# Squares summed in pairs, another order of norm and values, solves of three heads at a time: one core, one decoder trunk

## The chip, the cores and the metric

The kernel runs on one core of one Trainium2 chip. A core has a matrix engine (PE; its weight loads are listed apart as PEld), a vector engine (DVE), a scalar engine (ACT), a general engine (POOL) and an engine that here only issues transfers (SP). The first four work on tiles in SBUF; PE writes its results to PSUM, from where DVE and ACT read them. The metric is the device time of one launch in microseconds; less is better.

## The reference

The program is a two-layer decoder trunk over 512 positions of 1024 values, batch 1, in float32. Cut to what is computed:

```
mem_n = rms_norm(mem, ln_mem)                       # 256 memory tokens
for layer in (0, 1):
    h = rms_norm(x, ln_mix[layer])
    mem_k, mem_v = split(mem_n @ w_mem_kv[layer])   # both layers read the same memory
    if layer == 0:  mix, mem_q = gated_deltanet(h)  # 6 heads, chunked WY form
    else:           mix, mem_q = window_attention(h @ w_q, shared_k, shared_v)
    x = x + concat(mix, memory_attention(mem_q, mem_k, mem_v)) @ w_out[layer]
    x = x + swiglu(rms_norm(x, ln_ffn[layer]))
    if layer == 0:  shared_k, shared_v = rope / split of rms_norm(x, ln_kv) @ w_kv
return rms_norm(x, ln_final)
```

Here `rms_norm(x, g) = x * rsqrt(mean(x^2) + eps) * g`. The gated-DeltaNet layer needs, for every head and chunk of positions, the solution of a unit lower triangular system: `(I + lower) sol = rhs`. The kernel inverts the triangular matrices in blocks.

## The kernel before

Activations lie transposed: tile k of x holds 128 of the 1024 channels on the partitions and the 512 positions along the row, eight tiles in all. A large product is done in float32 by parts: each operand is split into a rounded high part and the rest (`split`: the high part is a copy on ACT, the low part a subtraction on DVE), and `mm3` issues three matmuls, high by high, high by low, low by high. A 128x1024 weight comes by one transfer (`wraw`), is split into `whi` and `wlo`, and feeds 24 matmuls. Weights wait in two raw buffers and three split ones (`whi`, `wlo`). Nobody writes the order of the engines by hand: a scheduler sets it from the program's order, from a model of the costs and from the buffers that are free, and each engine then works through its queue in that order. PSUM has eight banks, shared out by tag: in the first layer three `pj` (projections), two `g` and three `sc`.

The stages that the change touches are these.

*Early stage* (`mem_and_norm`, L279 to L363). Memory and weights are loaded, memory is split with its gain, `keys(0)` projects the first layer's memory keys (two tiles, 48 matmuls of 256 columns), `memory_stats` gets the norm of memory, `values(0)` projects the values (48 matmuls), `rstd_of` gets the norm of x, `norm` scales the eight tiles of x on DVE and splits them into `h` and `l`, and `keys(1)`, `values(1)` do the second layer's projections, which are kept in DRAM. Then `gates` projects two small gates from `h` and `l` (16 matmuls with `wabs`), and the projections of the first layer with a causal convolution begin (`conv_tile`).

`rstd_of` (L210) takes the sum of squares over the 1024 channels: each tile is squared on ACT into one of four `sq` buffers, and a plain float32 matmul with a matrix of ones adds it up over partitions and tiles in one `g` bank; two ACT steps (logarithm, exponential) make the inverse root. It runs once over memory (256 columns) and once over x (512).

*Solves* (`solve`, L650). For one head it turns four chunks' inverses of 32x32 blocks into inverses of 64 and then 128: products into an `sc` bank, a copy `Y` out of it on DVE, products with it into the same bank, and scalings by -1 into `X` and `Tt` on DVE. It does the two pairs of 32-blocks after each other and then the pair of 64-blocks. `values(heads)` (L560) inside `gdn` calls it for each of three heads and then does the three heads' value projections; the order is values of heads 0 to 2, their scan over four chunks, values of heads 3 to 5, their scan.

*End* (`ffn`, L897 to L909, and `final`, L1038). The last output tile of the last layer is done in two halves of 256 positions. For each half, x is added, squared on ACT, added on DVE to the running sum of squares `acc`, summed by one matmul with ones, turned into `rstd` by two ACT steps, and then `final` multiplies the eight tiles with gain and `rstd`: six on DVE (`fin`, one instruction each), two (`k0 == 4`) with the gain on ACT and `rstd` on POOL. Four output transfers per half follow.

Of the kernel before, what the change touches and what calls it, by code (L numbers as in the profile page):

```python
# [9 lines left out]
F32 = mybir.dt.float32  # L10
# [13 lines left out]
NC = 4  # L24
# [61 lines left out]
class Builder:  # L86
# [123 lines left out]
    def rstd_of(self, tiles, pool, out, after=None):  # L210

        ps = self.bank("g")[:, :tiles[0].shape[1]]
        for k, x in enumerate(tiles):
            sq = self.t(pool, [P, x.shape[1]], F32, "sq", 4)
            ins = self.square(sq, x)
            if after is not None:
                self.nosync(ins, after)
            self.mm(ps, self.ones, sq, k == 0, k == KD - 1)
        self.rsqrt(out, ps, D)
# [59 lines left out]
    def mem_and_norm(self, ep):  # L279
# [9 lines left out]
        for k in range(0, KD, 2):  # L289
            nc.sync.dma_start(mem[:, k:k + 2, :], a["memT"][:, k:k + 2, :])  # L290
            if k < 4:
                s = slice(k // 2 * T, (k // 2 + 1) * T)
                nc.sync.dma_start(raw[0][:, s], a["wmk"][0, 0][:, s])
        raw += [early(s) for s in (a["wmk"][0, 1], a["wmv"][0, 0], a["wmv"][0, 1])]
        self.fetch_constants()
        for k in range(KD):
            self.split_gain(mem[:, k, :], self.gain(G_MEM, k), mh[:, k, :], ml[:, k, :])
        for k in range(0, KD, 2):
            nc.sync.dma_start(x[:, k:k + 2, :], a["xT"][:, k:k + 2, :])
        wab = self.t(ep, [P, KD, 12], F32, "wab")  # L300
        nc.sync.dma_start(wab, a["wab"])
# [7 lines left out]
        def keys(layer):  # L309
            ps, ks = [], []  # L310
            for m in range(2):
                w = self.weight(None, nc.vector, raw[4 * layer + m], 1 if m + layer else 2)
                ps.append(self.bank("pj")[:, :ML])
                for k in range(KD):
                    self.mm3(ps[m], w, k, (mh[:, k, :], ml[:, k, :]), k == 0, k == KD - 1)
# [10 lines left out]
        def values(layer):  # L326
            vs = []
            w = [self.weight(None, nc.vector, raw[4 * layer + 2 + j]) for j in range(2)]
            for j in range(2):
                ps = self.bank("pj")[:, :ML]  # L330
                s = slice(j * P, (j + 1) * P)
# [21 lines left out]
        self.memK = keys(0)  # L353
        self.memV = values(0)
        self.rstd_of([x[:, k, :] for k in range(KD)], ep, xr)
        norm()
        w = self.wab = self.t(ep, [P, KD, 64], F32R, "wabs")
        nc.gpsimd.memset(w.bitcast(F32), 0.0)
# [96 lines left out]
    def gdn(self, gp):  # L455
# [104 lines left out]
        def values(heads):  # L560
            for h in heads:
                self.solve(gp, h, N[h], X, Tt[h])
            for h in heads:
                v = self.conv_tile(2 * H + h, self.t(gp, [P, T], F32, "qv", 5))
# [35 lines left out]

        first, second = range(0, 3), range(3, H)
        values(first)
        scan(first)
# [45 lines left out]

    def solve(self, gp, h, N, X64, Tt):  # L650

        X = X64[:, h * NC:(h + 1) * NC, :]
        B = BASE
        part = lambda ps, a, w: ps[:, a * w * NC:(a + 1) * w * NC].rearrange("p (c m) -> p c m", c=NC)
        ps = self.bank("sc")
        yx, rx, rt = (part(ps, a, B) for a in range(3))
        y = self.t(gp, [P, NC, B], F32, "Y32", 2)
        for a, b in ((slice(0, B), slice(B, 2 * B)), (slice(2 * B, 3 * B), slice(3 * B, 4 * B))):
            first = a.start == 0
            for c in range(NC):  # L660
                self.mm(yx[b, c, :], N[a, c, b], X[a, c, 0:B])
            self.nc.vector.tensor_copy(y[b], yx[b])
            for c in range(NC):
                if first:
                    self.mm(rx[b, c, :], Tt[b, c, b], y[b, c, :])
                self.mm(rt[a, c, :], y[b, c, :], Tt[b, c, b])
            if first:
                self.ts(X[b, :, 0:B], rx[b], -1.0, ALU.mult)
            self.ts(Tt[a, :, b], rt[a], -1.0, ALU.mult)
        ps = self.bank("sc")  # L670
        B = 2 * BASE
        yx, rt = (part(ps, a, B) for a in range(2))
        y = self.t(gp, [P, NC, B], F32, "Y64", 2)
        a, b = slice(0, B), slice(B, 2 * B)
        for c in range(NC):
            self.mm(yx[b, c, :], N[a, c, b], X[a, c, :])
        self.nc.vector.tensor_copy(y[b], yx[b])
        for c in range(NC):
            self.mm(rt[a, c, :], y[b, c, :], Tt[b, c, b])
        self.ts(Tt[a, :, b], rt[a], -1.0, ALU.mult)  # L680

# [180 lines left out]
    def ffn(self, fp, xp, layer, h, apool, rope=False):  # L862
# [34 lines left out]
        if tail < KD:  # L897

            w = {m: [down(m, j, n, pool=fp if m == KD - 1 and tail < KD - 1 else None) for j, n in ((0, 6), (6, 5))] for m in range(tail, KD)}
            for t in (slice(0, T // 2), slice(T // 2, T)):  # L900
                acc = self.acc[:, t]
                for m in range(tail, KD):
# [4 lines left out]
                    self.tt(nc.vector, x, ps, x, ALU.add)  # L907
                    self.accumulate(xp, acc, x, m, acc)
                self.final(fp, acc, t)  # L909

# [126 lines left out]

    def final(self, fp, acc, t):  # L1038

        nc = self.nc  # L1040
        self.rstd_from(acc, t)
        r = self.rstd[:, t]
        rows = self.a["out"].rearrange("(k p) t -> p k t", p=P)
        for k0 in range(0, KD, 2):
            o = self.t(fp, [P, 2, T // 2], F32, f"fin{k0}", 2)
            for k in (k0, k0 + 1):
                x, y = self.x[k][:, t], o[:, k - k0, :]
                if k0 == 4:
                    self.copy(y, x, scale=self.gain(G_FIN, k))
                    self.tt(nc.gpsimd, y, y, r, ALU.mult)  # L1050
                else:
                    self.stt(y, x, self.gain(G_FIN, k), r, ALU.mult, ALU.mult)
            nc.sync.dma_start(rows[:, k0:k0 + 2, t], o)
# [59 lines left out]
```

## Time and profile before

| | us |
|---|---|
| median of 3 runs | 1239.17 |
| lowest, highest | 1237.04, 1240.69 |
| profiled execution, its time | 1240.29 |
| profiled execution, its span | 1238.5 |
| PE busy | 1202.3 (97%) |
| DVE busy | 651.6 (53%) |
| ACT busy | 523.4 (42%) |
| POOL busy | 92.9 (8%) |
| PE idle before the first matmul | 6.0 |

The profile shows one execution. Busy time counts an instruction from start to modelled end, so neighbours on PE overlap in it; the distance from one start to the next is what an instruction costs in a stream. The mean granted clock of PE over the execution is 0.992 of full speed: it is 1.00 for most of the time and 0.50 in a few stretches. A line in a row can be that of a helper (L143 is every matmul, L150 every two-operand product or sum on POOL and DVE, L131 and L137 the ACT functions and copies), so the tiles' names tell the stage. In the chain of waits each piece is followed back from the last instruction to what released it; a name after `<-` in brackets is what ended an engine's idle time.

### The profile page before, as it was taken

Reading aid. Unit: us, or ns where it says so; the run is one execution under the profiler, and the core shown is the slowest. Engines: PE = TensorE matmul, PEld = TensorE weight load, DVE = VectorE, ACT = ScalarE, POOL = GpSimd, SP = SyncE. Lnnn points to the kernel's source line nnn. Section 1 sums busy time; section 2 is a strip of 40 time slices with the busy share of each in tenths; the row PEclk is TensorE's granted clock in tenths of the full one; section 3 lists DMA queues with packets and bytes.
Section 4 is the critical chain, followed back from the end, with each engine's and each line's share of the span. In section 5 each row is a group of like instructions: output and inputs, shape, how many; then the busy total and the mean of one; then the engine's idle time right before and its main releaser. Section 6 shows DMA issues by size and latency. Waiting matters only on the chain.

```text
span 1238.5 us, 15507 instructions
## 1 busy us (share of the span) xinstructions
PE 1202.3 (97%) x5963; PEld 984.7 (80%) x5963; DVE 651.6 (53%) x1116; ACT 523.4 (42%) x972; POOL 92.9 (8%) x63
## 2 busy tenths in 40 slices
PE   7899999999999999999999999989999999999996
PEld 6677777877888888888888888878888888888885
DVE  4554686667954433334435789967344333344344
ACT  6468375337442322222333557774323222223332
POOL 0120000000011110011110000000111100111001
PEclk9899999999999999999999999999999999999998
DMA  7332643223432223333333553304333233333232
GB/s 273 118 119 55 199 123 95 86 85 109 139 102 92 96 77 96 117 102 94 94 83 94 152 152 82 86 18 122 100 95 93 78 98 115 102 97 91 83 94 79
DMA packets 56798, 129.48 MB, mean 105 GB/s; under 512 B 15452, under 2 KB 19188, under 8 KB 56724
## 3 DMA queue, kind: packets, MB, share of 16 engines
q1 hardware_dynamic: 56724, 128.49, 34.8%
q8 instruction: 47, 0.77, 0.3%
q14 instruction: 27, 0.22, 0.1%
HBM read 113.12 MB, written 6.96 MB: 97 GB/s over the span
## 4 chain that ended last, share of the span: by engine, by line
PE 83%; ACT 5%; DVE 4%; DMA 2%; issue 1%; SPq 0%; DVEq 0%; ACTq 0%
PE pj L143 51%; PE g L143 25%; PE sc L143 5%; ACT sm L131 1%; DVE wlo L150 1%; PE g L147 1%; PE pt L147 1%; ACT whi L137 1%; ACT DT L131 1%; ACT h L137 0%; DVE fin L153 0%; DVE kn L153 0%; DMA wraw<-in_wq 0%; DVE l L153 0%; DMA wraw<-in_wout 0%
## 5 line engine op out<-in xcount | busy, mean ns | idle before, releaser
L137 ACT ACTIVATE whi<-wraw 128x1024 fp32r<-128x1024 f32 (+2 forms) x213 | 207.3, 975 | 546.4 <-PE pj L143 332.0
L143 PE MATMUL pj<-h,whi 128*128 128x512 f32 (+1 forms) x960 | 377.0, 394 | 2.1 <-ACT h L137 2.0
L143 PE MATMUL pj<-h,wlo 128*128 128x512 f32 (+1 forms) x960 | 374.8, 391 | 1.9 <-DVE wlo L150 1.9
L143 PE MATMUL pj<-l,whi 128*128 128x512 f32 (+1 forms) x960 | 375.6, 391 | 0.0
L150 DVE TENSOR_TENSOR wlo<-wraw,whi 128x1024 fp32r<-128x1024 f32 (+2 forms) x213 | 238.9, 1123 | 144.5 <-ACT whi L137 144.1
L143 PEld LDWEIGHTS pj<-h,whi 128*128 128x128 f32 x960 | 180.3, 188 | 39.0 <-ACT h L137 3.1
L143 PEld LDWEIGHTS pj<-h,wlo 128*128 128x128 f32 x960 | 180.5, 188 | 38.3 <-DVE wlo L150 2.6
L143 PEld LDWEIGHTS pj<-l,whi 128*128 128x128 f32 x960 | 180.6, 188 | 36.5 <-issue 1.0
L143 PE MATMUL g<-h,wlo 128*128 128x512 f32 x408 | 159.3, 390 | 0.6 <-DVE wlo L150 0.6
L143 PE MATMUL g<-l,whi 128*128 128x512 f32 x408 | 159.4, 391 | 0.0
L143 PE MATMUL g<-h,whi 128*128 128x512 f32 x408 | 159.2, 390 | 0.0
L150 POOL TENSOR_TENSOR fg<-fg,rstd 128x512 f32<-128x512 f32 x44 | 75.5, 1717 | 1009.6 <-ACT fg L131 1009.6
L150 DVE TENSOR_TENSOR fu<-g,fg 128x512 f32<-128x512 f32 x44 | 30.4, 691 | 142.6 <-PE g L143 139.9
L143 PEld LDWEIGHTS g<-h,wlo 128*128 128x128 f32 x408 | 76.8, 188 | 16.8 <-DVE wlo L150 1.0
L143 PEld LDWEIGHTS g<-l,whi 128*128 128x128 f32 x408 | 76.9, 188 | 16.0
L143 PEld LDWEIGHTS g<-h,whi 128*128 128x128 f32 x408 | 76.7, 188 | 15.8
L150 DVE TENSOR_TENSOR fg<-pj,rstd 128x512 f32<-128x512 f32 x44 | 30.4, 691 | 110.4 <-PE pj L143 110.2
L150 DVE TENSOR_TENSOR x<-pj,x 128x512 f32<-128x512 f32 (+1 forms) x41 | 27.8, 677 | 66.2 <-PE pj L143 66.1
L153 DVE SCALAR_TENSOR_TENSOR qv<-pj,gains,qv 128x511 f32<-128x511 f32 (+2 forms) x36 | 26.6, 740 | 7.1 <-ACT qv L137 6.8
L140 ACT ACTIVATE sq<-x 128x512 f32<-128x512 f32 (+1 forms) x41 | 24.8, 614 | 13.0 <-DVE x L150 10.9
L131 ACT ACTIVATE fg<-fg 128x512 f32<-128x512 f32 x44 | 27.7, 629 | 1.5 <-DVE fg L150 1.5
L137 ACT ACTIVATE h<-x,gains 128x512 fp32r<-128x512 f32 x32 | 22.1, 711 | 5.3 <-DVE x L150 5.3
(288 smaller groups left out, 1316.7 us busy)
## 6 DMA issues: line engine op xcount, KB each, us to landing
wraw<-in_wgu SPq DMA_DIRECT2D x88, 512.0 KB, 3.5
wraw<-in_win SPq DMA_DIRECT2D x26, 512.0 KB, 3.8
wraw<-in_wdn SPq DMA_DIRECT2D x32, 384.0 KB, 3.2
wraw<-in_wdn SPq DMA_DIRECT2D x32, 320.0 KB, 2.9
wraw<-in_wout SPq DMA_DIRECT2D x16, 512.0 KB, 4.0
wraw<-in_wq SPq DMA_DIRECT2D x8, 512.0 KB, 3.8
wraw<-in_wmv SPq DMA_DIRECT2D x4, 512.0 KB, 9.1
x<-in_xT SPq DMA_DIRECT2D x4, 512.0 KB, 9.7
```

The lines of the kernel that those rows point to most:

```text
L131: ins = self.nc.scalar.activation(out, in_, func, **kw).ins
L137: self.copied = self.nc.scalar.activation(out, in_, AF.Copy, **kw).ins
L140: return self.nc.scalar.activation(out, in_, AF.Square).ins
L143: self.nc.tensor.matmul(out, lhsT, rhs, start=start, stop=stop)
L147: self.nc.tensor.transpose(out, in_, self.ident[:k, :k])
L150: return eng.tensor_tensor(out=out, in0=a, in1=b, op=op).ins
L153: self.nc.vector.scalar_tensor_tensor(out=out, in0=in0, scalar=scalar, in1=in1, op0=op0, op1=op1)
```

## The change

- `rstd_of` squares two tiles, adds the second square to the first on DVE, and sums the pair by one matmul: four matmuls with ones in place of eight. The `sq` buffers are six instead of four.
- The norm of x and the scaling of x come ahead of `values(0)` in the program, and the transfers of the first layer's value weights come behind those of x.
- The second layer's keys and the first half of its values go to `sc` banks instead of `pj`.
- `solve` takes three heads at once and does each level (32, then 64) for all of them: products of both pairs and the copies for every head, then the products with the copies and the scalings for every head. Both groups' solves stand ahead of the first group's values in the program.
- At the end, `acc` and the square of the last tile are summed in PSUM by two matmuls, without the add on DVE. The two ACT steps write to PSUM, ACT copies the result to `rstd` for POOL, and DVE's products read it from PSUM. The pair for POOL is the first of the four.

```diff
@@ rstd_of
-        for k, x in enumerate(tiles):
-            sq = self.t(pool, [P, x.shape[1]], F32, "sq", 4)
-            ins = self.square(sq, x)
-            if after is not None:
-                self.nosync(ins, after)
-            self.mm(ps, self.ones, sq, k == 0, k == KD - 1)
+        for k in range(0, KD, 2):
+            two = []
+            for x in tiles[k:k + 2]:
+                sq = self.t(pool, [P, x.shape[1]], F32, "sq", 6)
+                two.append(sq)
+                ins = self.square(sq, x)
+                if after is not None:
+                    self.nosync(ins, after)
+            self.tt(self.nc.vector, two[0], two[0], two[1], ALU.add)
+            self.mm(ps, self.ones, two[0], k == 0, k == KD - 2)
@@ mem_and_norm
-        raw += [early(s) for s in (a["wmk"][0, 1], a["wmv"][0, 0], a["wmv"][0, 1])]
+        raw += [early(a["wmk"][0, 1])]
...
         for k in range(0, KD, 2):
             nc.sync.dma_start(x[:, k:k + 2, :], a["xT"][:, k:k + 2, :])
+        raw += [early(s) for s in (a["wmv"][0, 0], a["wmv"][0, 1])]
...
-                ps.append(self.bank("pj")[:, :ML])
+                ps.append(self.bank("sc" if layer else "pj")[:, :ML])
...
-                ps = self.bank("pj")[:, :ML]
+                ps = self.bank("pj" if j or not layer else "sc")[:, :ML]
...
         self.memK = keys(0)
-        self.memV = values(0)
         self.rstd_of([x[:, k, :] for k in range(KD)], ep, xr)
         norm()
+        self.memV = values(0)
@@ gdn
             for h in heads:
-                self.solve(gp, h, N[h], X, Tt[h])
-            for h in heads:
...
+        for heads in (first, second):
+            self.solve(gp, heads, [N[h] for h in heads], X, [Tt[h] for h in heads])
         values(first)
@@ solve, new
+        for B, starts in ((BASE, (0, 2 * BASE)), (2 * BASE, (0,))):
+            pairs = [(slice(s, s + B), slice(s + B, s + 2 * B)) for s in starts]
+            banks = [self.bank("sc") for _ in heads]
+            ys = [self.t(gp, [P, NC, B], F32, f"Y{B}", 3) for _ in heads]
+            for ps, N, X, y in zip(banks, Ns, Xs, ys):
+                for a, b in pairs:
+                    for c in range(NC):
+                        self.mm(part(ps, 0, B)[b, c, :], N[a, c, b], X[a, c, 0:B])
+                for a, b in pairs:
+                    nc.vector.tensor_copy(y[b], part(ps, 0, B)[b])
+            for ps, X, y, Tt in zip(banks, Xs, ys, Tts):
+                for a, b in pairs:
+                    for c in range(NC):
+                        if B == BASE and a.start == 0:
+                            self.mm(part(ps, 1, B)[b, c, :], Tt[b, c, b], y[b, c, :])
+                        self.mm(part(ps, 2 if B == BASE else 1, B)[a, c, :], y[b, c, :], Tt[b, c, b])
+                for a, b in pairs:
+                    if B == BASE and a.start == 0:
+                        self.ts(X[b, :, 0:B], part(ps, 1, B)[b], -1.0, ALU.mult)
+                    self.ts(Tt[a, :, b], part(ps, 2 if B == BASE else 1, B)[a], -1.0, ALU.mult)
@@ ffn
-                    self.accumulate(xp, acc, x, m, acc)
-                self.final(fp, acc, t)
+                sq = self.t(fp, [P, T // 2], F32, "sql", 2)
+                self.square(sq, x)
+                self.final(fp, (acc, sq), t)
@@ final
-        self.rstd_from(acc, t)
+        self.use(LN_EXP)
+        ps = self.bank("g")[:, t]
+        for k, sq in enumerate(squares):
+            self.mm(ps, self.ones, sq, k == 0, k == len(squares) - 1)
+        self.fn(ps, ps, AF.Ln, scale=1.0 / D, bias=self.eps)
+        self.fn(ps, ps, AF.Exp, scale=-0.5)
         r = self.rstd[:, t]
+        self.copy(r, ps)
...
-        for k0 in range(0, KD, 2):
+        for k0 in (4, 0, 2, 6):
...
-                    self.stt(y, x, self.gain(G_FIN, k), r, ALU.mult, ALU.mult)
+                    self.stt(y, x, self.gain(G_FIN, k), ps, ALU.mult, ALU.mult)
```

More of the change, by code (lines that the diff above doesn't have):

```diff
@@ L648, in base_inverse, with solve @@
         return X64, [Tt[:, h * NC:(h + 1) * NC, :] for h in range(H)]
-    def solve(self, gp, h, N, X64, Tt):
-        X = X64[:, h * NC:(h + 1) * NC, :]
-        B = BASE
+    def solve(self, gp, heads, Ns, X64, Tts):
+        nc = self.nc
+        Xs = [X64[:, h * NC:(h + 1) * NC, :] for h in heads]
         part = lambda ps, a, w: ps[:, a * w * NC:(a + 1) * w * NC].rearrange("p (c m) -> p c m", c=NC)
[L655 to L680, printed above, removed]
@@ L1036, in swa, with final @@
         return [mix[t] for t in range(KD)]
-    def final(self, fp, acc, t):
+    def final(self, fp, squares, t):
         nc = self.nc
-        self.rstd_from(acc, t)
+        self.use(LN_EXP)
[4 more added lines that the diff above has]
+        self.fn(ps, ps, AF.Exp, scale=-0.5)
         r = self.rstd[:, t]
+        self.copy(r, ps)
         rows = self.a["out"].rearrange("(k p) t -> p k t", p=P)
-        for k0 in range(0, KD, 2):
+        for k0 in (4, 0, 2, 6):
             o = self.t(fp, [P, 2, T // 2], F32, f"fin{k0}", 2)
```

## The prediction

> **What bounds the kernel now.** I read the page first, then the waits of the matrix engine (PE) alone, then stretches of the stages that the diff touches. Columns of the stretches: from and to, length, busy time of PE, its weight loads, DVE, ACT and POOL with instruction counts, granted clock, DMA share, GB/s.
>
> ```profile
> span 1238.5 us, 15507 instructions
> PE 1202.3 (97%) x5963; PEld 984.7 (80%) x5963; DVE 651.6 (53%) x1116; ACT 523.4 (42%) x972; POOL 92.9 (8%) x63
> ```
> ```profile
> PE pj L143 <- DVE kt L150: 4.0, 1, 4.0
> PE g L143 <- DVE sqa L150: 3.4, 1, 3.4
> ```
> ```profile
> 18.08:21.34 3.26, 3.26 (x18) 2.87 (x17) 0.00 (x0) 2.57 (x6) 0.00 (x0) 1.00 1.04 419
> 28.05:34.51 6.46, 6.46 (x18) 2.87 (x17) 2.69 (x3) 4.44 (x7) 0.00 (x0) 1.00 0.40 102
> 42.50:46.49 3.99, 0.00 (x1) 0.00 (x0) 3.99 (x8) 1.69 (x4) 0.00 (x0) 1.00 0.00 0
> 47.40:54.20 6.80, 6.20 (x30) 5.91 (x29) 3.59 (x4) 1.48 (x2) 0.00 (x0) 0.50 0.41 133
> 119.07:122.48 3.41, 1.78 (x12) 1.27 (x10) 3.12 (x9) 3.41 (x14) 0.00 (x0) 1.00 0.34 49
> 829.04:832.45 3.41, 1.74 (x10) 1.37 (x10) 1.17 (x3) 0.76 (x2) 0.00 (x0) 1.00 0.00 0
> 832.45:835.86 3.41, 3.41 (x10) 2.65 (x9) 2.11 (x4) 2.86 (x4) 0.00 (x0) 0.50 0.00 0
> ```
> PE is the bound: 97% busy. So what counts is PE work that disappears, PE idle time that closes, and the granted clock. The waits say that of the little idle there is, the two largest pieces after the first load lie where the diff edits: 4.0 us in the early stage and 3.4 us before the last sum. The stretches show what the sums of squares cost: the eight of memory 3.26 us, so 0.41 each; the eight of x 6.46 us, so 0.81 each; PE does nothing else meanwhile. After the 3.99 us idle the clock is 0.50 for 6.80 us: some 3.4 us more lost.
>
> **Early stage.**
>
> ```profile
> 21.65 0.28 PE L143 MATMUL pj<-whi,ml 128*128 128x256 f32 x1
> 21.77 0.29 PE L143 MATMUL pj<-wlo,mh 128*128 128x256 f32 x1
> 22.01 0.46 ACT L131 ACTIVATE mr<-g,eps 128x256 f32<-128x256 f32 x1
> 23.34 0.60 PE L143 MATMUL g<-consts,mr 1*128 1x1 f32 x4
> 28.62 1.05 ACT L137 ACTIVATE whi<-wraw 128x1024 fp32r<-128x1024 f32 x1
> 35.12 0.69 ACT L131 ACTIVATE xr<-g,eps 128x512 f32<-128x512 f32 x1 [2.43 <-PE g L143]
> 36.50 2.08 DVE L153 SCALAR_TENSOR_TENSOR x<-x,gains,xr 128x512 f32<-128x512 f32 x3 [3.59 <-ACT xr L131]
> 38.50 1.29 DVE L150 TENSOR_TENSOR l<-x,h 128x512 fp32r<-128x512 f32 x2
> 39.70 0.75 DVE L153 SCALAR_TENSOR_TENSOR x<-x,gains,xr 128x512 f32<-128x512 f32 x1
> 31.68 1.23 DVE L150 TENSOR_TENSOR wlo<-wraw,whi 128x1024 fp32r<-128x1024 f32 x1 [0.76 <-ACT whi L137]
> 46.02 0.74 DVE L150 TENSOR_TENSOR kt<-pj,mr 128x256 f32<-128x256 f32 x2
> 57.68 0.40 PE L143 MATMUL pj<-l,wabs 128*64 128x512 f32 x1
> 57.91 0.40 PE L143 MATMUL pj<-h,whi 128*128 128x512 f32 x1
> ```
> The prices, from start to start: 0.12 us for a 256-wide split matmul at full clock, 0.23 for a 512-wide one, 1.05 for a weight's high half on ACT, 1.23 for its low half on DVE, 0.66 for scaling a tile of x, 0.60 for its low half. The wait before 46.49 came about so: the second layer's values need a PSUM bank that a `kt` product frees, and that product (46.02) stood behind x and l on DVE. With `sc` banks for the second layer it has no such wait.
>
> Eight sums go (4 x 0.41 + 4 x 0.81 = 4.9 us of PE). In their place come eight adds on DVE: 4 of 256 and 4 of 512 columns, 0.37 and 0.6 each by the rows of `kt` and `l`, 3.9 us. All but the last run under the sums before them. What it costs is order. In the built program PE goes from the first keys to four memory sums, two one-column products, four sums of x, and only then to the first values. The keys still end at 18.08.
>
> - Four memory sums: to 19.7. Then ACT's two steps with one square between, 1.33 us from the start of the first to PE's next work (22.01 to 23.34 now): 21.1. PE waits 1.4 us here, a new wait. The one-column products take 0.60: 21.7. Four sums of x: 24.9.
> - The last transfer of x must have landed by 21. Each takes 9.7 us from its issue, the last is issued by 12.3, so 22 now; 1 MB fewer is queued ahead, at 419 GB/s 2.5 us: 19.5. It does not bind. The two transfers for the values, moved behind x, land 2.5 us after it, by 22; ACT turns to them at 23, behind the last square and the halves of the keys.
>
> ```profile
> x<-in_xT SPq DMA_DIRECT2D x4, 512.0 KB, 9.7
> 8.30 3.96 SPq L299 DMA_DIRECT2D x<-in_xT  x4
> ```
> - ACT must split both weight tiles of the first values (2 x 1.05) before the logarithm for x; they end at 25. The logarithm starts at 25.1 (35.12 now), scaling at 26.5 (36.50 now).
> - DVE then runs 8 scalings, 6 low halves and the low half of the next key weight before PE can resume its split matmuls: 8 x 0.66 + 6 x 0.60 + 1.23 = 10.1 us, to 36.6. Beside it PE has the values (48 x 0.12 = 5.8 us), eight matmuls taken ahead and 13 of the gates' 16 (3.0 us), and idles for some 2.5 us in three pieces (10.1 less 5.8, 8 x 0.12 and 3.0 is 0.3; the rest because the values start 1.6 before the scalings).
> - From 36.6 PE has 88 matmuls at 0.12 and 3 at 0.23 left, 11.3 us, nothing late: 47.9. A dozen hand-overs at 0.05 add 0.6: the first convolution starts at 48.6 instead of 57.91. **-9.3 us.** Check: 4.9 + 4.0 + 3.4 (clock) are freed, 1.4 + 2.5 are new: -8.4, and the 0.60 of PE idle within the stretch at 47.40 goes too: -9.0. Bounds: -4.9 (only the sums go) and -11.5 (only the first new wait stays). All that follows to the solves keeps its order, and PE is nearly full there, so the shift is passed on.
>
> **Solves.**
>
> ```profile
> 202.88 0.43 PE L143 MATMUL sc<-X,N 32*32 32x32 f32 x8
> 203.24 0.50 PE L143 MATMUL pj<-h,whi 128*128 128x512 f32 x1
> 203.58 0.40 PE L143 MATMUL pj<-l,whi 128*128 128x512 f32 x1
> 206.09 0.39 PE L143 MATMUL pj<-h,whi 128*128 128x512 f32 x1
> 206.41 0.21 PE L143 MATMUL sc<-Y,Tt 32*32 32x32 f32 x1
> ```
> The number of matmuls is the same. But each change from wide to small tiles and back costs: the first wide one after a block lasts 0.34, the last before one 0.32, instead of 0.23, together 0.20. In the built order PE is taken from projections to solves 14 times instead of 24: 10 x 0.20 = **-2.0 us**. The second group's solves move ahead of the first scan, which loses these fillers; there the other two heads' 128-wide matmuls still stand between a product and its use. The waits that this could bring are not in the trace; the nearest are
>
> ```profile
> PE g L143 <- DVE N L153: 0.7, 2, 0.4
> ```
> so at four level ends 4 x 0.4: from -0.4 to -2.5 (every mixed block too). I take -2.0 because PE has 0.6 to 2.7 us of other heads' or projection work at every level end.
>
> **Last sum.**
>
> ```profile
> 1222.68 0.71 PE g L143 x2
> 1224.43 3.52 DVE fin L153 x6
> 1229.24 1.24 PE g L143 x2
> 1231.01 0.43 ACT rstd L131
> ```
> ```profile
> 1224.47 1.60 POOL L150 TENSOR_TENSOR fin<-fin,rstd 128x256 f32<-128x256 f32 x2 [62.74 <-ACT rstd L131]
> 1226.29 1.66 DVE L153 SCALAR_TENSOR_TENSOR fin<-x,gains,rstd 128x256 f32<-128x256 f32 x4
> 74.15 2.31 DVE L153 SCALAR_TENSOR_TENSOR kn<-pj,gains,kn 128x511 f32<-128x511 f32 x3
> 68.10 8.53 POOL L150 TENSOR_TENSOR DT<-gcr,consts 128x512 f32<-128x512 f32 x6 [8.92 <-DMA gcr<-dr]
> ```
> In each half an add (0.37 by `kt`, and a hand-over) leaves the path. The extra sum of `acc`, 0.41 by the price above, runs before the square is ready. `fin` now reads PSUM: beside POOL two of them took 1.86 us, alone 0.395 each; `kn`, which reads PSUM too, keeps 0.77 with POOL running. So six take 2.4 instead of 3.5. Against it stands a copy to `rstd`, 0.46 by the 256-wide `mr` row; in the built program both DVE and POOL wait for it. First half: sum at 1222.25, copied by 1224.4, products to 1226.85 instead of 1227.95. Second: add, square, sum (0.71 at full clock) to 1228.5, two steps and the copy to 1229.95; now POOL and DVE start behind the second step (1231.01 + 0.43 = 1231.44). SP sends POOL's pair first, before and after, so the new order of the pairs costs nothing and the transfers follow POOL: **-1.5 us**. It is -1.0 if the sum runs at 1.24 as now, and -2.6 at most, if the transfers follow the products on DVE (1.1 shorter).
>
> **The clock.** Two pieces of idle that summed to 1.67 in 3.41 us (829.04) brought 0.50 for the next 3.41; 1.63 idle (119.07) did not. The new wait of 1.4 us plus the thin products (0.60) is at that edge. [...] One lost window costs 1.7 us, two 3.4.
>
> **Sum.** -9.3 - 2.0 - 1.5 = -12.8. The profiled execution took 1240.29 us (span 1238.5 and 1.8 around it): **1227.5 us**. That execution lies 1.1 above the median of 1239.17, within the 3.7 that the three runs span.
>
> **The rivals.**
> - The clock falls at the new waits: 1229.2 to 1230.9. For: the row at 829.04. Against: 119.07.
> - DVE and ACT take turns on x worse than I string them, and PE waits longer at 36.6: the early gain shrinks to the 4.9 us of sums removed, the solves give 0.4: -6.8, 1233.5. For: the trip of x and l takes DVE from 36.50 to past 46.02 now. Against: half of its stops were other weights.
> - The change doesn't do what it says: the bank wait closes, but PE waits for x's norm as long as that and the sums take now; the early gain is 0 and -3.5 is left: 1236.8, within 0.3%. For: PE now stands still through the whole norm of x. Against: the chain worked out above, in which the norm ends 10 us earlier.
> - Slower: with three heads a level, PE stands before DVE's copies and scalings at each of four level ends, and the clock falls each time (1.7). All told it needs 3.2 us a level to eat 12.8, and over 4.1 for slower than 0.3%; at 4.5 it is 1245.5. For: PE is in order and the solves now all stand before the first scan. Against: 0.4 us, the longest such wait now.
>
> **How the numbers follow.** Forecast 0.55, clock 0.22, turns 0.13, no net gain 0.05, slower 0.05. 0.3% (3.7 us) is about what a measurement here can tell from no change; the first three cases are all under 1235.4: faster 0.90, same 0.05, slower 0.05. The range leaves the last two out and the edges of the terms: 1223.5 (-9.3, -2.5, -2.6 and the spread of the runs) to 1233.
>
> **What would show it.** First convolution matmul near 48.6; a wait of 1.4 us near 20 on ACT's `mr`; no 4 us wait on `kt`; clock 1.00 from 25 to 50. First small-tile solve near 194, end of the second group's solves before the first scan, no wait over 0.4 there. `fin` at 0.4 us each beside POOL; last POOL pair 1.5 us earlier relative to the end of the projections. Wrong, if a wait over 3 us stands in the early stage, or the clock is 0.50 for two windows there.

## The result, and the profile after

The changed kernel takes 1224.84 us (median, 1222.3 to 1226.04) beside 1238.88 us (1237.04 to 1240.69) for the kernel before on the same chip: ratio 0.9884, 95% interval 0.9861 to 0.9907, so 14 us less. The profiled execution took 1225.75 us with a span of 1224.0. First the two lines of the page, then three of the waits of the matrix engine (PE), and one row of the kernel before that has not been shown yet.

```profile
span 1224.0 us, 15503 instructions
PE 1189.8 (97%) x5951; PEld 976.7 (80%) x5951; DVE 650.7 (53%) x1122; ACT 523.6 (43%) x974; POOL 92.3 (8%) x63
```
```profile
...
PE g L143 <- DMA qv<-mq0l: 2.0, 1, 2.0
...
PE g L143 <- ACT mr L131: 1.5, 1, 1.5
...
PE g L143 <- ACT sql L140: 0.9, 1, 0.9
```
```profile
PE g L143 <- DMA qv<-mq0l: 1.1, 1, 1.1
```

PE is as full as before and has 12.5 us less to do. The 4.0 us wait on `kt` is gone, and the 3.4 us wait of the last sum has become 0.9. The wait for `mr`, the inverse root for memory, is new. The wait for the transfer of `mq0l`, a low part of the first layer's memory query (near 142 us), has grown by 0.9 in this execution: it is 1.0 to 2.2 long in the executions of all these kernels.

PE's timeline of the early stage, changed kernel (start, length, instruction; in brackets the idle time ahead of it):

```profile
16.78 1.89 PE L143 MATMUL g<-sq,consts 128*128 128x256 f32 x8
20.13 0.60 PE L143 MATMUL g<-consts,mr 1*128 1x1 f32 x4 [1.46 <-ACT mr L131]
20.66 3.70 PE L143 MATMUL g<-sq,consts 128*128 128x512 f32 x8
...
31.14 0.38 PE L143 MATMUL sc<-whi,mh 128*128 128x256 f32 x1 [0.55 <-ACT whi L137]
...
34.91 0.44 PE L143 MATMUL pj<-h,wabs 128*64 128x512 f32 x1 [0.25 <-ACT h L137]
36.05 0.39 PE L143 MATMUL sc<-mh,wlo 128*128 128x256 f32 x1 [0.69 <-DVE wlo L150]
...
47.40 0.40 PE L143 MATMUL pj<-h,whi 128*128 128x512 f32 x1
```

Four sums of memory and four of x stand where sixteen stood (a plain float32 product makes two records, so four sums are x8); one wait of 1.46 near 20 and three small ones of 1.5 together follow, and the first convolution starts at 47.40 instead of 57.91. On ACT, the logarithm of x's norm:

```profile
24.39 0.69 ACT L131 ACTIVATE xr<-g,eps 128x512 f32<-128x512 f32 x1 [0.44 <-PE g L143]
```

It stood at 35.12. Now two stretches, each for the kernel before and after it for the changed one: from the first sum to the first transposition of `kn` (the early stage with the first convolution), and from the first small-tile solve to the last product of the scans. The columns are those of the stretches in the prediction.

```profile
18.08:70.87 52.79, 48.20 (x259) 38.83 (x257) 25.81 (x42) 27.76 (x50) 7.71 (x7) 0.94 0.47 153
...
202.88:296.65 93.77, 92.75 (x750) 73.12 (x749) 62.88 (x130) 39.85 (x86) 0.00 (x0) 1.00 0.27 85
```
```profile
16.78:61.17 44.39, 40.87 (x245) 33.16 (x243) 30.34 (x48) 26.70 (x47) 7.61 (x7) 1.00 0.58 192
...
194.60:282.49 87.89, 86.76 (x750) 70.12 (x750) 62.15 (x130) 40.14 (x86) 0.00 (x0) 1.00 0.28 91
```

The early stretch is 8.4 us shorter: PE is busy 7.3 less (the sums, and a mean clock of 1.00 instead of 0.94) and idle 1.1 less. The solves and scans are 5.9 shorter, with the same 750 matmuls at the same clock. The whole difference of the two spans goes down the program like this, by the starts of the same instructions in both: -1.3 ahead of the first sum; -8.4 to the first transposition of `kn`; +1.5 from there to the first attention, where a half-clock stretch that the execution before did not have (below) costs 1.6 and the wait for `mq0l` 0.9 more, a wait of 0.6 went, and 0.4 less was not followed up; -5.9 in solves and scans; +2.0 in the rest of both layers, where two half-clock stretches stand against one; -2.4 from the last projection matmul on. Sum -14.5.

The end of the changed kernel, DVE, POOL and PE:

```profile
1211.79 2.44 DVE L153 SCALAR_TENSOR_TENSOR fin<-x,gains,g 128x256 f32<-128x256 f32 x6 [2.60 <-ACT rstd L137]
1211.83 1.44 POOL L150 TENSOR_TENSOR fin<-fin,rstd 128x256 f32<-128x256 f32 x2 [62.57 <-ACT rstd L137]
...
1213.45 0.28 PE L143 MATMUL pj<-ac10h,wlo 128*128 128x256 f32 x1
...
1215.06 0.70 PE L143 MATMUL g<-sql,consts 128*128 128x256 f32 x2 [0.90 <-ACT sql L140]
...
1217.14 1.41 POOL L150 TENSOR_TENSOR fin<-fin,rstd 128x256 f32<-128x256 f32 x2 [3.87 <-ACT rstd L137]
```

Six `fin` products take 2.44 with POOL running beside them (3.52 before), and the sum of the second half takes 0.70 (1.24 before, at half clock). From the last projection matmul's start (1213.45; 1225.60 before) to the span's end it is 10.5 us instead of 12.9.

### The profile page after: what moved, and what is told of

Read it like the earlier page. It is cut to its first block, busy times and chain, and to the rows that moved or that the text cites. A ratio compares the mean times of both kernels' runs of the same rounds, so it can differ in the third digit from the quotient of the medians.

```text
span 1224.0 us, 15503 instructions
## 1 busy us (share of the span) xinstructions
PE 1189.8 (97%) x5951; PEld 976.7 (80%) x5951; DVE 650.7 (53%) x1122; ACT 523.6 (43%) x974; POOL 92.3 (8%) x63
## 4 chain that ended last, share of the span: by engine, by line
PE 87%; ACT 5%; DVE 4%; DMA 1%; issue 1%; SPq 0%; DVEq 0%; ACTq 0%
PE pj L143 55%; PE g L143 26%; PE sc L143 5%; PE pt L147 1%; DVE wlo L150 1%; PE g L147 1%; ACT whi L137 1%; DMA wraw<-in_wmk 1%; ACT sm L131 1%; ACT DT L131 1%; DVE l L150 0%; ACT sq L140 0%; DVE x L153 0%; ACT h L137 0%; DMA qv<-mq0l 0%
## 5 line engine op out<-in xcount | busy, mean ns | idle before, releaser
L143 PEld LDWEIGHTS g<-h,wlo 128*128 128x128 f32 x408 | 76.7, 188 | 17.3 <-DVE wlo L150 1.4
L140 ACT ACTIVATE sq<-x 128x512 f32<-128x512 f32 x39 | 24.1, 624 | 6.6 <-DVE x L150 3.9
```

The source lines that it names most:

```text
L140: return self.nc.scalar.activation(out, in_, AF.Square).ins
L143: self.nc.tensor.matmul(out, lhsT, rhs, start=start, stop=stop)
```

## The experiments

### Each part alone

Three kernels, each the kernel before with one part of the change (the hunks of the diff for `rstd_of` and `mem_and_norm`; for `gdn` and `solve`; for `ffn` and `final`).

> The kernel before with the early part alone (squares in pairs, norm ahead of the first values, sc banks); solves and last sum as before. The prediction's step: first convolution matmul at 48.6 us, -9.3. The two traces: 47.4 and about -10.5 there, of which 1.2 lie ahead of the first sum and go with the clock at the start, so 48.6 again if that was chance of one execution and 47.4 if not. [...] In all about -8.2, ratio 0.9934; without any clock loss -10, 0.992.

> The kernel before with the solves level by level alone. Excursions only (the prediction's step): -2.0 in the stage of the solves, ratio 0.998. Small matmuls of different rows and columns of the array run side by side when they stand together (read from the traces): -4.2 more, -6.2 in that stage; then by the window rule the two waits of the second attention's end each lie across two windows and the half-clock window near 832 goes as well, 1.7 more: -7.9, ratio 0.9936. Without the window rule -6.2, 0.995.

> The kernel before with the last sum in PSUM alone. The prediction's step: -1.5, ratio 0.9988; bounds -1.0 to -2.6. The two traces: the stretch from the last projection matmul to the end goes from 12.4 to 10.0, so -2.4, ratio 0.9981. If that 2.4 was in part a gift of the other parts (another phase of the clock at the end), it is -1.5 or less here. fin is 0.39 us from start to start beside POOL.

The window rule in these and later expectations is the author's estimate from the two first profiles. There 3.41 us at a clock of 0.50 followed stretches of 3.41 us with 1.61, 1.71 and 1.95 us of PE idle time (changed kernel, 805.14, 815.38 and 108.83) and with 1.67 and 2.50 (before, 829.04 and 43.99), and none followed one with 1.63 (before, 119.07).

| part alone | median, before | ratio (95%) | as us |
|---|---|---|---|
| early | 1231.51, 1238.5 | 0.9939 (0.9923 to 0.9956) | -7.6 (-9.5 to -5.4) |
| solves | 1231.73, 1238.5 | 0.9939 (0.9924 to 0.9953) | -7.6 (-9.4 to -5.8) |
| last sum | 1236.61, 1238.5 | 0.9983 (0.9974 to 0.9993) | -2.1 (-3.2 to -0.9) |

By time the solves gain as much as the early stage. (The three add up to -17.3, the whole change gives -14.4; the intervals are too wide to call that a loss.) Their stretch, in the kernel with the solves alone:

```profile
201.14:289.35 88.21, 86.97 (x749) 70.15 (x749) 62.10 (x130) 40.05 (x86) 0.00 (x0) 1.00 0.29 90
```

88.2, as in the changed kernel, against 93.8 to 94.4 in every execution with the old solves. So -5.6 to -6.2 is the change's own there; the -2.0 of excursions alone falls. The interval of the time, -9.4 to -5.8, holds most of that; what the rest of the -7.6 is, no run shows.

The early part: the first convolution at 47.49, the stretch to `kn` 44.3. But the executions of the other two kernels, whose early code is that of the kernel before, show what was chance in the first profile. Their first sums come at 16.3 and 16.2, where the kernel before had 18.08, the latest of all these executions. The -1.3 at the start is not the change's. Their stretches to `kn` are 51.2 and 52.1 (52.8 before): the 4 us wait was there each time, but once it cost one half-clock stretch instead of two.

The last sum alone: from the last projection matmul (1223.86) to the end (1234.4) 10.5, as in the changed kernel, and by time -2.1. (The expectation counts to half a microsecond ahead of the span's end: its 12.4 is the 12.9 of the result, its 10.0 the 10.5.) The 12.9 itself was in part chance. In four of the five other executions with the old end the second half's sum takes 0.70, at full clock, and that stretch is 12.4; here with the early part alone:

```profile
1219.93 0.70 PE L143 MATMUL g<-sqa,consts 128*128 128x256 f32 x2 [3.36 <-DVE sqa L150]
```

So the change's own is about -1.9, which the -2.1 fits; the other 0.5 is half clock that the first profile happened to have.

### Which piece of the early part

Again the kernel before, with one piece each.

```diff
 banks alone
-                ps.append(self.bank("pj")[:, :ML])
+                ps.append(self.bank("sc" if layer else "pj")[:, :ML])
...
-                ps = self.bank("pj")[:, :ML]
+                ps = self.bank("pj" if j or not layer else "sc")[:, :ML]
 pairs alone: rstd_of as in the changed kernel
 order alone, with the transfers of the first value weights behind x
-        self.memV = values(0)
         self.rstd_of([x[:, k, :] for k in range(KD)], ep, xr)
         norm()
+        self.memV = values(0)
```

> The kernel before with sc banks for the second layer's keys and first value alone; sums and order as before. The prediction's step: the 3.99 us wait of PE on kt goes, and with it the half-clock time that followed it: -4.0 to -7.4, first convolution matmul at 50.5 to 54 in place of 57.9, ratio 0.994 to 0.997. Rival: the low half of the second layer's weights stands behind x and l on DVE as kt did, and PE waits for that instead, about as long: 0 to -1, ratio 0.999 or more.

> The kernel before with the squares added in pairs alone; order and banks as before. The prediction's step: 8 of 16 sums go, 4 x 0.41 + 4 x 0.81 = 4.9 us less of PE; xr, x, l and kt come as much earlier, and the 4 us wait on kt stays: -4.9, ratio 0.996, the two groups of sums 1.7 and 3.3 us long. Rival: the end of the early stage is set by ACT's squares and DVE's x and l, which the sums only lie beside: the groups get shorter and PE waits in them for the squares: -2 or less, ratio over 0.998.

> The kernel before with the norm of x ahead of the first values (and the transfers in that order) alone; 16 sums and the pj banks as before. If the order is what lets DVE be done with x and l in time, the wait on kt shrinks to under 1 us and its half-clock time goes: -4 to -6 less about 3 for the new waits at the two norms, so -1 to -3, ratio 0.998 to 0.999. Rival: the bank is what binds, the 4 us wait stays at its place and the new waits come on top: +2 to +3, ratio 1.002.

Banks 0.9948 (0.9931 to 0.9965), -6.4 us; pairs 0.9962 (0.9948 to 0.9976), -4.7; order 1.0003 (0.9991 to 1.0016), nothing. The three apart give -11, together -7.6; where the rest goes is shown in the section after this one. First the stretch to `kn` with the banks alone; then, with the pairs alone, the same stretch and PE's only wait in it; then, with the order alone, two rows of PE's timeline:

```profile
17.35:63.16 45.81, 45.59 (x261) 36.49 (x259) 25.94 (x43) 27.63 (x51) 7.44 (x6) 1.00 0.55 180
```
```profile
17.46:64.59 47.13, 42.33 (x244) 35.36 (x242) 28.96 (x47) 26.26 (x46) 7.87 (x7) 0.93 0.53 177
```
```profile
PE pj L143 <- DVE kt L150: 4.8, 1, 4.8
```
```profile
22.23 0.60 PE L143 MATMUL g<-consts,mr 1*128 1x1 f32 x4 [1.65 <-ACT mr L131]
...
42.11 0.43 PE L143 MATMUL pj<-mh,wlo 128*128 128x256 f32 x1 [2.50 <-DVE wlo L150]
```

With the banks alone PE has 0.2 us of idle time in 45.8: the bank was what bound, and the rival (another wait as long) falls. The expectation's mark of 50.5 to 54 for the first convolution says nothing, because PE takes its steps in another order there and the first convolution starts at 47.1; the `kn` mark does. With the pairs alone the wait on `kt` stays, and even grows to 4.8. With the order alone the wait on `kt` goes, but a wait of 1.65 on `mr` and one of 2.50 on a low half take its place: no gain.

### The order taken back

If the order gains nothing and costs waits, the changed kernel should be better without it.

```diff
 the changed kernel, with
-        self.rstd_of([x[:, k, :] for k in range(KD)], ep, xr)
-        norm()
         self.memV = values(0)
+        self.rstd_of([x[:, k, :] for k in range(KD)], ep, xr)
+        norm()
 and the transfers of the first value weights ahead of x again
```

> The changed kernel with the first values ahead of the norm of x again, and the transfers in that order; pairs, sc banks, solves and last sum stay. If the order costs (order alone: the stretch from the first sum to the first transposition of kn is 54.9 against 52.8 before, new waits of 1.6 at mr and of 2.5 at wlo) and the banks alone leave PE without a wait (45.8), the eight sums come off that: 41 to 42 against 44.4 in the changed kernel, -2.5 to -3.5, ratio 0.9855 to 0.9865 against before. Rival, the prediction's chain: norm ahead of the values is what lets DVE be done with x and l in time; without it PE waits 2 us or more for the second layer's weights or the first convolution's, the stretch is 44.4 or longer and the ratio 0.988 or more.

Median 1221.22 beside 1238.36: ratio 0.9867 (0.9847 to 0.9888). The stretch to `kn`:

```profile
16.08:57.82 41.74, 40.88 (x245) 33.49 (x244) 29.53 (x48) 26.37 (x49) 8.00 (x6) 1.00 0.61 211
```

41.7 with the same 40.9 of PE work as in the changed kernel (44.4), so 2.7 us less idle: the expected size. (The 54.9 in the expectation misled, since with the order alone the first sum itself comes earlier, at 13.66; the waits did not.) By time the two intervals overlap; the traces show the 2.7, the times do not settle it. The stretch also says where the three pieces lose: with the old early code the stretch is 52.0 on average (below), with the banks alone 6.2 less, with the pairs alone 4.9 less, with both 10.3 less. These two nearly add up, and the order takes 2.7 of it back.

### Why the solves gained three times the forecast

One block of products as it runs: the kernel before, then the changed kernel (start, length, instruction; the next row tells when PE goes on).

```profile
202.88 0.43 PE L143 MATMUL sc<-X,N 32*32 32x32 f32 x8
203.24 0.50 PE L143 MATMUL pj<-h,whi 128*128 128x512 f32 x1
```
```profile
194.60 1.20 PE L143 MATMUL sc<-X,N 32*32 32x32 f32 x48
195.73 0.50 PE L143 MATMUL pj<-h,whi 128*128 128x512 f32 x1
```

Eight took 0.36 from start to start, 48 take 1.13 and not six times 0.36. There are two candidates: fewer ends of blocks, or products of different rows and columns of the array that run side by side. They can be told apart by the order of the 48 records (24 products, two records each): they are twice 24 of the same rows and columns, and stand in the changed kernel as 8 and 8 in alternation.

```diff
 the changed kernel, with
-            for ps, N, X, y in zip(banks, Ns, Xs, ys):
-                for a, b in pairs:
+            for a, b in pairs:
+                for ps, N, X in zip(banks, Ns, Xs):
                     for c in range(NC):
                         self.mm(part(ps, 0, B)[b, c, :], N[a, c, b], X[a, c, 0:B])
 and the products with y, three kinds, in the same way
```

> The changed kernel with the solves' products ordered so that 24 (three heads by four chunks by two, or by one) of the same rows and columns of the array stand together, in place of 8 and 8 in alternation; same number, same banks, same three heads a level, as many changes between wide and small tiles. Side by side theory: small matmuls of different rows and columns overlap, those of the same do not; the 240 products of 32x32, 5.2 us from start to start in the changed kernel and 8.7 before, become some 7.5 to 8: +2 to +3 in that stage, ratio 0.990 to 0.991 against before. Excursions only: the stage stays as long as in the changed kernel, ratio 0.988.

The same block, and the stretch of solves and scans:

```profile
194.90 1.60 PE L143 MATMUL sc<-X,N 32*32 32x32 f32 x48
196.43 0.50 PE L143 MATMUL pj<-h,whi 128*128 128x512 f32 x1
```
```profile
194.90:284.35 89.45, 88.32 (x749) 71.68 (x749) 62.23 (x130) 40.16 (x86) 0.00 (x0) 1.00 0.29 89
```

1.53 for the 48, 0.032 each, and 89.45 instead of 87.89: +1.5, less than the 2 to 3 expected. In the alternating block many records start 0.005 or 0.006 after the one ahead, in this one nearly all 0.03. Side by side is real, but only part. From start to start over the stage, all small products take 16.3 us before, 13.4 here and 11.9 in the changed kernel. So of 4.4 us, 1.5 come from products of different rows and columns running side by side, and 2.9 from longer blocks. The records show what a block's end costs: from a 32x32 record to the next one it is 0.03 on average, to a wide or a 64x64 one 0.12 (64x64: 0.07 and 0.15). There are 39 such ends before and 15 after, so the 24 that went make some 2.1 of the 2.9; the other 0.8 lies between neighbours within the blocks. The projections of the same stage take 1.8 less, which is the forecast's own term, and the 128-wide products 0.3 more. The ratio, 0.9917 (0.9895 to 0.9939), is on the side of the first theory, but it holds more than the stage: three of its four executions ran at a mean clock of 0.990 or 0.991, where those of the changed kernel had 0.993 to 0.996. The stage decides. So the rows above give 0.4 us per 48 records for the alternation (1.13 against 1.53) and 0.09 more at each end of a block of 32x32 products (0.12 against 0.03).

### The read of PSUM

```diff
 the changed kernel, with
-                    self.stt(y, x, self.gain(G_FIN, k), ps, ALU.mult, ALU.mult)
+                    self.stt(y, x, self.gain(G_FIN, k), r, ALU.mult, ALU.mult)
```

> The changed kernel with the products of fin on DVE reading rstd in SBUF in place of the sum in PSUM; the copy, the sums and all orders stay. Contention theory: the two of six that run beside POOL take 1.86 together in place of 0.79, the first half's six end 1.0 to 1.1 later, the second half's add starts as much later, and POOL's two take 1.6 in place of 1.4: the stretch from the last projection matmul to the end goes from 10.0 to 11.2 or 11.3. If what the last sum gained was only the add that went and the clock, fin takes 0.39 each here too and the stretch stays 10.0.

```profile
1211.52 3.53 DVE L153 SCALAR_TENSOR_TENSOR fin<-x,gains,rstd 128x256 f32<-128x256 f32 x6 [2.60 <-ACT rstd L137]
1214.97 0.41 DVE L150 TENSOR_TENSOR x<-pj,x 128x256 f32<-128x256 f32 x1
1217.92 3.49 DVE L153 SCALAR_TENSOR_TENSOR fin<-x,gains,rstd 128x256 f32<-128x256 f32 x6 [2.54 <-ACT rstd L137]
```

Six products take 3.53 again, the second half's add (1214.97) waits for them, and from the last projection matmul (1213.19) to the end of the span (1225.0) it is 11.8 instead of 10.5: +1.3. So 1.3 of the last sum's gain comes from reading PSUM beside POOL. The time, 1226.75, is one execution.

### The clock

Apart from the start and the end, the profile of the changed kernel has three half-clock stretches of 3.41 us, that of the kernel before as many; where they fell differs. Within one trace they begin whole multiples of 3.41 us apart: that is the grid in what follows. The first try to move them:

```diff
 the changed kernel, with, ahead of the first convolution's first matmul
+        for _ in range(again):   # 4
+            self.mm(ps, w[0][:, 0:P], acts[0][0])
```

> The changed kernel with four matmuls more, whose product is written over at once, ahead of the first convolution: 0.92 us of work for nothing, 4 x 0.23. Window rule: the waits near 112, 808 and 818, which each lie in one window of 3.41 us in the changed kernel and are each followed by a half-clock window, move by 0.9 and each fall across two windows; none of the three windows is lost: +0.9 - 3 x 1.6 = -3.9 against the changed kernel, about 1221. If the clock falls for the length of the wait, wherever it lies, or at random: +0.9, about 1225.7, with the same half-clock windows.

Median 1224.93, ratio 0.9883 (0.9862 to 0.9904): neither 1221 nor clearly more than the changed kernel, though the stretch to `kn` is 45.4, longer by the 0.97 put in. Two of the three half-clock stretches are still there, at 113.6 and 816.8. Here is the wait near 110 in four executions, each as a stretch of 3.41 us and the next one: the changed kernel; this one; the early part alone; the pairs alone. The last two rows are the wait on `mr`, in the kernel whose `fin` reads SBUF.

```profile
108.83:112.24 3.41, 1.46 (x11) 1.02 (x10) 3.18 (x9) 3.41 (x13) 0.00 (x0) 1.00 0.32 48
112.24:115.66 3.42, 3.42 (x9) 2.64 (x10) 0.94 (x1) 3.09 (x11) 0.00 (x0) 0.50 0.77 206
```
```profile
110.23:113.64 3.41, 1.46 (x7) 0.89 (x7) 3.19 (x6) 3.41 (x13) 0.00 (x0) 1.00 0.38 55
113.64:117.06 3.42, 3.42 (x10) 2.65 (x9) 0.20 (x1) 2.35 (x9) 0.00 (x0) 0.50 0.88 277
```
```profile
108.49:111.90 3.41, 1.80 (x12) 1.29 (x11) 3.09 (x9) 3.41 (x13) 0.00 (x0) 1.00 0.34 48
111.90:115.32 3.42, 3.07 (x13) 2.55 (x14) 1.43 (x2) 3.42 (x13) 0.00 (x0) 1.00 0.70 190
```
```profile
114.77:118.18 3.41, 1.70 (x7) 1.43 (x8) 2.79 (x5) 3.41 (x13) 0.00 (x0) 1.00 0.36 55
118.18:121.60 3.42, 3.42 (x17) 2.82 (x15) 0.00 (x0) 1.56 (x6) 0.00 (x0) 1.00 0.89 299
```
```profile
17.74:21.15 3.41, 0.65 (x6) 0.56 (x5) 1.59 (x3) 3.30 (x7) 0.00 (x0) 1.00 1.03 409
21.15:24.56 3.41, 3.41 (x5) 1.45 (x5) 2.89 (x6) 3.19 (x6) 0.00 (x0) 0.50 0.95 357
```

The same wait of 1.95 lies whole in one stretch of 3.41 us and drops the clock (PE busy 1.46 of it), or lies across two (1.80, 1.70) and does not; these two had 1.61 and 1.71 idle, which is at the edge, as the count below shows. Where the stretches begin differs from execution to execution of the same early code (counted back from 108.83, one begins at 20.1 in the changed kernel's first profile; in its second, below, one begins at 21.2), so "the same places" falls: the four matmuls moved the wait, and the grid had moved as well. The size of the idle time counts. In the 14 traces of this study there are 67 stretches on that grid at full clock, from 15 to 1200 us, with at least 1.0 us of PE idle time: under 1.6 idle the clock fell after 1 of 29, at 1.60 to 1.73 after 18 of 23, from 1.86 on after 15 of 15.

> The changed kernel once more, beside the next one on the same chip. The early stretch from the first sum to the first transposition of kn 44.4 (47 where the clock falls at the wait on mr), the stage of the solves and scans as in its first profile, 87.9, ratio 0.988. Half-clock windows at other places than in its first profile if their phase is chance, at the same places (112, 808, 818) if it is not.

The changed kernel once more: 1224.5 beside 1238.46, ratio 0.9881 (0.9862 to 0.9900). Its half-clock stretches are at 21.2, 809.7 and 819.9, not at 112, 808.6 and 818.8. The last two follow the same two waits in both executions, the first another one; the early stretch is 46.6, since this time the clock fell at the wait on `mr`. That happened in 2 of 6 executions with the changed early stage (46.6 and 47.1 to `kn`, 44.3 to 44.6 in the other four, the 0.92 of idle work left out).

### Filling a wait

```diff
 the kernel with the order taken back, with
-        return self.project(self.a["win"][m], self.h)
+        return self.project(self.a["win"][m], self.h, again=6 if m == 3 * H + 4 else 0)
...
-        for k0 in (4, 0, 2, 6):
+        for k0 in (0, 4, 2, 6):
```

> The changed kernel with the first values ahead of the norm of x again, and two things more: the first of DVE's pairs of fin is sent ahead of POOL's pair, and six matmuls for nothing (written over at once) stand ahead of the fifth gate projection, before the 1.95 us wait on wlo. Against the kernel with the first values ahead alone (ratio 0.9867): the pair of DVE is ready 0.55 us before POOL's, so the last stretch goes from 10.0 to 9.4; the wait shrinks from 1.95 to about 0.55, and no half-clock window can follow it, which saves 1.7 in the executions (6 of 12 so far) where one did: -0.55 and some -0.8, ratio 0.9855. Rival: the wait is not for DVE alone, the six matmuls come on top: +1.4, and transfers set the end whichever pair goes first: ratio 0.988.

Median 1223.97, ratio 0.9871 (0.9850 to 0.9892): no difference to the kernel with the order taken back (0.9867) can be told. The second edit came to nothing: the first transfer still starts behind POOL's products (1211.81, these end at 1211.78), and the last stretch stays 10.5, so that was not tried. The first did what it should at its place, by PE's waits in the first 115 us:

```profile
PE pj L143 <- DVE wlo L150: 0.6, 1, 0.6
```

The wait is 0.6 instead of 1.95 and no half-clock stretch follows. But in this execution the one for `mq0l` lay whole in one stretch (2.0 idle at 138) and dropped the clock there.

## Why the prediction was right, and where it was not

The time came out inside the range, 2.7 us below the forecast: 1.4 of it because the forecast starts from an execution of 1240.29 and the median is 1238.88, 1.2 because the change gives more. Of its three terms one held in the first two profiles and is some 2 us too large over all executions, one was a third of what it should be, and one was a little small.

| term | forecast (bounds) | the two profiles | the part alone, by time |
|---|---|---|---|
| early stage | -9.3 (-4.9 to -11.5) | -9.2 to the first convolution, -8.4 to `kn` | -7.6 (-9.5 to -5.4) |
| solves | -2.0 (-0.4 to -2.5) | -5.9 | -7.6 (-9.4 to -5.8) |
| last sum | -1.5 (-1.0 to -2.6) | -2.4 | -2.1 (-3.2 to -0.9) |
| elsewhere | 0 | +2.2 (start, clock, `mq0l`) | |
| sum | -12.8 | -14.5 | 0.9884: -14.4 (-17.2 to -11.5) |

**Early stage.** The steps held nearly one by one: a wait of 1.46 on `mr` near 20 (1.4 forecast), the logarithm for x at 24.4 (25.1; from the first sum 7.6 and not 7.0), three later waits of 1.5 together (2.5), no wait on `kt`, clock 1.00 throughout; from the first sum, the first convolution comes 9.2 earlier. What was wrong is to take the half-clock time of one execution, 3.4 us, as a fixed part of the kernel before, and the fall of the clock at the new wait as a rival with a chance of its own. Both differed from execution to execution: the old wait cost one half-clock stretch or two, and the new one cost one in 2 of 6. Over the executions at hand the stretch to `kn` is 51.2 to 52.8 with the old early code and 44.3 to 47.1 with the new, means 52.0 and 45.2: -6.8, with which the -7.6 by time agrees. The forecast also did not ask which piece gives the gain. It is the bank and the sums; the order, on which its longest chain of steps was spent, costs 2.7.

**Solves.** The step that failed is "the number of matmuls is the same. But each change from wide to small tiles and back costs", priced at the wide matmuls alone. That price held: the projections take 1.8 less. Left out was the small side: the end of each block of small products (0.12 in place of 0.03, and also between 32 and 64), and products that run side by side, together 4.4. The range of the term, -0.4 to -2.5, did not hold it, because its lower end was built from the same kind of row. The rows of the trace were there: eight products in 0.36 are 0.045 each, and one product followed by another of its kind 0.03.

**Last sum.** The mechanism held: no add, `fin` at 0.4 each beside POOL, transfers behind POOL's pair. The size was 0.9 small in the profile: the first half was done 0.55 earlier against the last projection matmul than the chain had it, the two steps and the copy took 1.3 instead of 1.45, POOL's two products 1.4 instead of 1.6. But 0.5 of the -1.5, the sum at full clock, was again the half clock of one execution taken as fixed: against the executions without it the term is -1.0 forecast and -1.9 measured.

**The rivals.** That the clock falls at the new waits is no case of its own: it happened in 2 of 6 executions. DVE and ACT taking turns on x (1233.5): the waits after 25 us sum to 1.5, so no. No net gain: the norm of x did end 10 us earlier (37.2 against 47.5). Waits at the level ends of the solves: PE is idle for 1.1 us in the whole stretch of 87.9, and was for 1.0 before. In the two profiles the solves' extra 3.9 and the last sum's 0.9 made up for the 0.9 that the early stage lacks to `kn` and the 2.2 elsewhere; that the sum came this close was in part luck.

**The clock.** The expectations of the early part, of the solves and of the four matmuls count 1.6 to 1.7 us for each half-clock stretch by the window rule; no run shows it as a rule. The runs showed the count above (the clock fell after 1 of 29 stretches with under 1.6 us of PE idle time, after 18 of 23 with 1.60 to 1.73, after 15 of 15 from 1.86 on), and 1224.93 where the four matmuls were to bring 1221.

## What to carry to other kernels

Price a change between tile sizes on both sides: what the wide matmul pays and what the last small one before it pays (here 0.20 for the two wide neighbours of a block, and 0.09 at the end of 32x32 products), and put small products of different rows and columns next to each other (here 48 records took 1.13 so and 1.53 in turn). Before crediting a change with a wait or a half-clock stretch that one execution shows, ask how often it falls: here a wait of 1.6 to 3.4 us of PE cost its own length, and up to 1.7 more (3.41 us at a clock of 0.50) where nearly half of one 3.41 us window or more was idle: after 18 of 23 windows with 1.60 to 1.73, 15 of 15 from 1.86 on and 1 of 29 with less than 1.6. The place of the windows differed from execution to execution (20.1 and 21.2 in two of the changed kernel). A wait for a PSUM bank that is freed only behind a long queue on DVE (4.0 us) was removed here by another bank; another order of the work put other waits (1.65 and 2.50) in its place.

## What was not expected

The order alone gave nothing and, once the bank was free, cost 2.7 us of PE idle time: a step moved ahead to be early for one engine made another stand still. And a faster start does not help what follows at once. In the kernel whose `fin` reads SBUF the early code is the changed kernel's, and the first sum came at 15.93 instead of 16.78:

```profile
15.93 1.89 PE L143 MATMUL g<-sq,consts 128*128 128x256 f32 x8
20.58 0.60 PE L143 MATMUL g<-consts,mr 1*128 1x1 f32 x4 [2.76 <-ACT mr L131]
```

PE waited 2.76 instead of 1.46 and went on at 20.58 instead of 20.13: what it reached earlier it spent on the wait, and the clock fell behind it (0.50 from 21.15 to 24.56).
